# Half of a 31-tap depthwise convolution computed on VectorE instead of TensorE, with gates and output products in another order

## The chip, the cores and the metric

The kernel runs on one core of a Trainium2 chip. The metric is the device time of one execution in microseconds (us). A core has five engines that run beside each other, each with its own in-order queue: PE (TensorE, matrix products), DVE (VectorE), ACT (ScalarE), POOL (GpSimd) and SP (SyncE, which here issues the DMA transfers). Arrays on the chip have 128 partitions; results of PE arrive in PSUM, which has eight banks.

## The reference, cut to what matters

The program is two model blocks for 512 tokens of 1024 features, all in fp32. The change lies in the second block's mixer. Its input projection gives a convolution branch (u_glu), a state space branch (z, xbc, dt) and 2048 gates. The convolution branch is a causal depthwise convolution with 31 taps over 1024 channels:

```python
def conformer_conv_branch(u_glu, glu_b, dw_w, dw_b, ln_g, ln_b, pw_w, pw_b):
    u = u_glu + glu_b
    val, gt = jnp.split(u, 2, axis=-1)
    v = val * jax.nn.sigmoid(gt)
    v = causal_depthwise_conv(v, dw_w, dw_b)          # 31 taps, 1024 channels
    v = jax.nn.silu(layer_norm(v, ln_g, ln_b))        # over all 1024 channels
    return v @ pw_w + pw_b
...
        gates = jax.nn.sigmoid(proj[..., OFF_GATE:] + gate_b[i])
        g_conv, g_ssm = jnp.split(gates, 2, axis=-1)
        conv_out = conformer_conv_branch(...)
        ssm_out = ssd_branch(...)                     # ends in y @ out_w
        mixed = (g_conv * conv_out + g_ssm * ssm_out) @ w_out[i]
```

## The kernel before

Features lie on partitions: a channel tile is 128 channels by 512 tokens, and the convolution has eight of them. Every large product is taken in three matmuls of split operands (mm3, L125): each weight tile of 128x1024 is split by ACT into a high part (L119, L1661) and by POOL into a low part (L121, L1663), with three buffers of each. One projection (proj, L1694) is such a split and 24 matmuls of 512 columns into one PSUM bank; the banks of tag g are two.

The mixer (phase3, L1667) first runs eight groups. Group gi is glu(gi), group(gi) and conv(gi). glu (L1752) is two projections and the gated value vp (L1763); it copies vp into vs, four shifted copies of each block of 32 channels (16 transfers), and builds a block-diagonal weight dw on DVE (L1772). group (L1787) is six projections, a 4-tap convolution on DVE (L1806, L1809) for four of them, and the state space product of four heads, with steps on PE, DVE, ACT and POOL that wait for each other; it ends in two channel tiles of y, stored to memory (L1908). conv (L1776) is 64 matmuls that use 32 columns of PE each, four side by side (L1782), and an evacuation into cv (L1784). The groups' temporary tiles are all in one pool, gw, closed at L1915.

Then come, in the order of the text: the layer norm of cv over channels (L1918 to L1943: a sum over the eight tiles on POOL, a product with ones on PE, centring, squares, a second product with ones, scaling and a silu); sixteen gate projections, whose tanh (L1952) is stored to memory (L1953); the state space branch's out product (gemm_krow, L205, 16 tiles k, with all eight PSUM banks as accumulators), which loads y and the gates back (L1969, L1974); the convolution branch's pointwise product (8 tiles k); and the product with w_out. The out product's inputs are split on ACT and DVE (L224, L226). Around it the residual h is loaded and scaled on DVE (L2005).

The text does not fix the order of the queues. A planner that runs when the program is built simulates it and gives each engine, whenever it is idle there, the ready instruction that stands earliest in the text. Two things tie an order: issue_after (this instruction behind that one in its queue) and keep_in_program_order, which in_order (L191) applies to all of PE's instructions in its scope. A pool opened in the space of a closed pool waits until all of the closed pool is released.

```python
        dw = wk.tile([P, 8, 4, 32], F32, name="dw", tag="dw", bufs=1)
        ...
                nc.tensor.matmul(ps[32 * b:32 * b + 32, :], dw[:, i, b], vs[:, b, 4 * i:4 * i + T],
                                 start=(i == 0), stop=(i == 7), tile_position=(0, 32 * b))
```

Of the kernel before, what the change touches and what calls it, by code (L numbers as in the profile page):

```python
# [109 lines left out]
def split(g, w, shape, pool=None, after=None, hi_on=None):  # L110
# [9 lines left out]
    with tc.issue_after(after[1].ins) if after else nullcontext():  # L120
        (nc.vector if after else nc.gpsimd).tensor_tensor(lv, w, hv, op=OP.subtract)  # L121
# [1459 lines left out]
def p3_loads(g, I, pool):  # L1581
# [4 lines left out]
    for name, items in (  # L1586
# [64 lines left out]
def split_cols(g, w, c, m=P, pool=None):  # L1651
# [10 lines left out]
    with g.tc.issue_after(g.last_hp.ins):  # L1662
        nc.gpsimd.tensor_tensor(wl, wv, wh, op=OP.subtract)  # L1663
# [3 lines left out]
def phase3(g, I, h, out, dbg):  # L1667
# [35 lines left out]
    cv = cvp.tile([P, 8, T], F32, name="cv")  # L1703
    ln_st = ExitStack()
# [4 lines left out]
    gd = [g.dram.tile([P, T], F32, name=f"gTd{i}") for i in range(16)]  # L1709
# [42 lines left out]
    def glu(ct):  # L1752
# [6 lines left out]
        nc.scalar.activation(vb, pv, AF.Identity, bias=tb[:, o_glu + ct:o_glu + ct + 1])  # L1759
        vp = wk.tile([P, 31 + T], F32, name="vp", tag="vp")  # L1760
# [4 lines left out]
        vs = wk.tile([P, 4, VW], F32, name="vs", tag="vs", bufs=1)  # L1765
# [5 lines left out]
        w4 = tdw[ct // 4].rearrange("p (i c) -> p i c", i=8)[:, :, 4 * (ct % 4):4 * (ct % 4) + 4]  # L1771
# [4 lines left out]
    def conv(ct, vd):  # L1776
# [7 lines left out]
        nc.scalar.activation(cv[:, ct], ps, AF.Identity, bias=tb[:, o_dwb + ct:o_dwb + ct + 1])  # L1784

# [133 lines left out]
    nc.gpsimd.tensor_tensor(s1, cv[:, 0], cv[:, 1], op=OP.add)  # L1919
    for k in range(2, 8):  # L1920
        nc.gpsimd.tensor_tensor(s1, s1, cv[:, k], op=OP.add)
    pm = pp.tile([P, 512], F32, name="pln", tag="m")
    nc.tensor.matmul(pm, g.ones, s1, start=True, stop=True)
    s2 = lnp.tile([P, T], F32, name="lns2", tag="s")
    for k in range(8):
        V.scalar_tensor_tensor(cv[:, k], pm, -1.0 / D, cv[:, k], op0=OP.mult, op1=OP.add)
        sq = s2 if k == 0 else lnp.tile([P, T], F32, name="lnsq", tag="t")
        nc.scalar.activation(sq, cv[:, k], AF.Square)
        if k:
            V.tensor_add(s2, s2, sq)  # L1930
    pm = pp.tile([P, 512], F32, name="pln", tag="m")
    nc.tensor.matmul(pm, g.ones, s2, start=True, stop=True)
    rs = lnp.tile([P, T], F32, name="lnr", tag="s")
    nc.scalar.activation(rs, pm, AF.Ln, bias=g.epsl, scale=1.0 / D)
    nc.scalar.activation(rs, rs, AF.Exp, scale=-0.5)
    for k in range(8):
        V.tensor_mul(cv[:, k], cv[:, k], rs)
        th = lnp.tile([P, T], F32, name="lnth", tag="t")
        nc.scalar.activation(th, cv[:, k], AF.Tanh, scale=half[:, o_lng + k:o_lng + k + 1],
                             bias=half[:, o_lnb + k:o_lnb + k + 1])  # L1940
        nc.scalar.activation(cv[:, k], cv[:, k], AF.Identity, scale=tb[:, o_lng + k:o_lng + k + 1],
                             bias=tb[:, o_lnb + k:o_lnb + k + 1])
        V.scalar_tensor_tensor(cv[:, k], th, 1.0, cv[:, k], op0=OP.add, op1=OP.mult)  # L1943
# [12 lines left out]

# [8 lines left out]
    ktp = kt_st.enter_context(tc.tile_pool(name="kt", bufs=2, side="right"))  # L1965

    def yget(k):
        t = ktp.tile([P, T], F32, name="yk", tag="yk", bufs=4)
        nc.sync.dma_start(t, yd[k][:, :])  # L1969
        return t  # L1970

    def gget(i):
        t = ktp.tile([P, T], F32, name="gk", tag="gk", bufs=13)
        nc.sync.dma_start(t, gd[i][:, :])  # L1974
        return t

    gts = {}

    def so_evac(i, ps):
        if dbg is not None and "ssm" in dbg:  # L1980
            t = ktp.tile([P, T], F32, name="dbt", tag="pwt")
            V.tensor_copy(t, ps)
            nc.sync.dma_start(dbg["ssm"][i * P:(i + 1) * P, :], t)
        V.scalar_tensor_tensor(mix[:, i], gts[8 + i], 1.0, ps, op0=OP.add, op1=OP.mult)

    def pw_evac(i, ps):
        t = ktp.tile([P, T], F32, name="pwt", tag="pwt")
        nc.scalar.activation(t, ps, AF.Identity, scale=0.5, bias=tb[:, o_pwb + i:o_pwb + i + 1])
        if dbg is not None and "conv" in dbg:
            nc.sync.dma_start(dbg["conv"][i * P:(i + 1) * P, :], t)  # L1990
# [192 lines left out]
```

## Time and profile before

| | us |
|---|---|
| median of 3 runs (lowest to highest) | 2046.89 (2046.56 to 2046.96) |
| the profiled execution: time | 2046.73 |
| the profiled execution: span from the first to the last instruction | 2045.0 |
| PE busy | 1979.2 |
| DVE busy | 961.5 |
| ACT busy | 702.4 |
| POOL busy | 749.1 |

The rows further down come from one profiled execution. A row's busy time counts from an instruction's start to its end, and ends of neighbours on one engine overlap a little, so that a row of several has less than the sum of its instructions. An idle time is put down to what ended last before the engine went on. A source row gives the least, the median and the largest duration in ns and the first and last start.

### The profile page before, as it was taken

The page shows a single profiled execution, that of the slowest core. Times are in us where ns is not written, and L with a number is a line of the kernel's source. Part 1 is how long each engine was busy: PE and PEld are TensorE (multiplying, and loading weights), DVE is VectorE, ACT ScalarE, POOL GpSimd, SP SyncE. Part 2 cuts the span into 40 slices and gives each one's busy share as a digit, 9 for nine tenths or more (in the row PEclk, how much of TensorE's full clock was granted, in tenths as well). Part 3 has the DMA queues.
Part 4 walks back from the last instruction along what each step waited for, and adds up shares of the span by engine and source line. Part 5 has one row for each costly group of instructions (what it writes and reads, how often), then busy time and mean ns, then how long its engine had stood idle before and what let it go on. Part 6 is the DMA issues. An engine that isn't in the chain of part 4 may idle for free.

```text
span 2045.0 us, 25143 instructions
## 1 busy us (share of the span) xinstructions
PE 1979.2 (97%) x9841; PEld 1396.8 (68%) x9841; DVE 961.5 (47%) x1500; ACT 702.4 (34%) x1057; POOL 749.1 (37%) x490
## 2 busy tenths in 40 slices
PE   7999989799999999989999999999999999999998
PEld 6877637644445545468777777778788888888886
DVE  6266475733444334346776667773545671000112
ACT  5344574411111111153433344443542452222232
POOL 4455453200000000044565555546344444444442
PEclk9999999799999999999999999999999999999999
DMA  4311216299999999845335444434653343332321
GB/s 141 124 42 42 83 42 237 97 399 411 420 420 419 419 419 419 318 140 137 105 114 145 115 118 124 121 106 145 217 184 127 110 113 84 103 98 88 103 83 42
DMA packets 186659, 366.73 MB, mean 179 GB/s; under 512 B 18000, under 2 KB 128888, under 8 KB 161960
## 3 DMA queue, kind: packets, MB, share of 16 engines
q1 hardware_dynamic: 186040, 363.43, 50.0%
q8 instruction: 79, 1.29, 0.3%
q10 hardware_dynamic: 496, 1.64, 0.3%
q14 instruction: 44, 0.36, 0.1%
HBM read 343.54 MB, written 12.65 MB: 174 GB/s over the span
## 4 chain that ended last, share of the span: by engine, by line
PE 64%; DVE 9%; ACT 3%; issue 2%; POOL 2%; SPq 0%; DMA 0%; DVEq 0%; ACTq 0%; POOLq 0%
PE pgu L197 11%; PE psg L126 7%; PE psg L127 7%; PE psg L128 7%; PE py L197 6%; PE pc L197 3%; PE px L197 3%; DVE xacc L1809 2%; PE pcv L1782 2%; DVE G L1878 1%; PE acctr L126 1%; PE accy L126 1%; PE acctr L127 1%; PE acctr L128 1%; PE accy L127 1%
## 5 line engine op out<-in xcount | busy, mean ns | idle before, releaser
L126 PE MATMUL psg<-xh,hi 128*128 128x512 f32 x1040 | 411.5, 396 | 2.5 <-DVE z L1823 2.4
L128 PE MATMUL psg<-xh,lo 128*128 128x512 f32 x1040 | 409.2, 393 | 1.5 <-POOL lo L121 1.5
L127 PE MATMUL psg<-xl,hi 128*128 128x512 f32 x1040 | 406.3, 391 | 0.0
L1663 POOL TENSOR_TENSOR lo<-w,hi 128x1024 fp32r<-128x1024 f32 (+1 forms) x125 | 305.6, 2447 | 239.5 <-ACT hi L1661 233.0
L121 POOL TENSOR_TENSOR lo<-w,hi 128x1024 fp32r<-128x1024 f32 x86 | 210.8, 2456 | 225.8 <-ACT hi L119 224.8
L1661 ACT ACTIVATE hi<-w 128x1024 fp32r<-128x1024 f32 (+1 forms) x125 | 131.1, 1051 | 325.2 <-PE psg L127 227.0
L197 PE MATMUL pgu<-w,xg 128*64 128x512 f32 x1024 | 227.6, 599 | 0.0
L128 PEld LDWEIGHTS psg<-xh,lo 128*128 128x128 f32 x1040 | 195.3, 188 | 44.9 <-issue 2.8
L127 PEld LDWEIGHTS psg<-xl,hi 128*128 128x128 f32 x1040 | 195.4, 188 | 44.2 <-issue 4.7
L126 PEld LDWEIGHTS psg<-xh,hi 128*128 128x128 f32 x1040 | 195.4, 188 | 43.8 <-DVE z L1823 3.4
L1334 POOL TENSOR_TENSOR hh<-x,hh 128x512 fp32r<-128x512 f32 x4 | 5.1, 1275 | 459.6 <-ACT hh L1333 459.6
L197 PEld LDWEIGHTS pgu<-w,xg 128*64 128x64 f32 x1024 | 73.1, 138 | 144.3 <-issue 141.8
L119 ACT CAST hi<-w 128x1024 fp32r<-128x1024 f32 x89 | 92.9, 1044 | 149.5 <-issue 54.8
L197 PE MATMUL py<-w,aT 128*64 128x512 f32 x512 | 113.6, 596 | 0.2 <-ACT aT L1467 0.2
L2105 DVE TENSOR_TENSOR act<-act,psg 128x512 f32<-128x512 f32 x22 | 15.1, 688 | 208.3 <-PE psg L128 203.0
L1459 DVE TENSOR_TENSOR act<-act,pgu 128x512 f32<-128x512 f32 x16 | 11.0, 688 | 187.4 <-PE pgu L197 187.4
L1809 DVE SCALAR_TENSOR_TENSOR xacc<-xp,tsc,xacc 128x512 f32<-128x512 f32 x96 | 90.7, 944 | 2.4
L1322 DVE TENSOR_TENSOR x<-x,pc 128x512 f32<-128x512 f32 x120 | 75.8, 682 | 15.1 <-PE pc L197 14.8
L197 PEld LDWEIGHTS py<-w,aT 128*64 128x64 f32 x512 | 35.4, 137 | 67.6 <-issue 65.4
L1490 ACT ACTIVATE yh<-py,gsl 128x512 fp32r<-128x512 f32 x32 | 22.0, 687 | 138.0 <-PE py L197 138.0
L1806 DVE TENSOR_SCALAR xacc<-xp,tsc,tb 128x512 f32<-128x512 f32 x32 | 49.1, 1534 | 41.5 <-ACT xp L1804 37.0
L1881 POOL TENSOR_TENSOR G<-G,cb 128x512 f32<-128x512 f32 x32 | 50.3, 1588 | 40.0 <-ACT G L1880 25.7
(789 smaller groups left out, 3648.1 us busy)
## 6 DMA issues: line engine op xcount, KB each, us to landing
w<-in_w_expert_down_dram SPq DMA_DIRECT2D x64, 1024.0 KB
w<-in_w_expert_gate_dram SPq DMA_DIRECT2D x64, 1024.0 KB
w<-in_w_expert_up_dram SPq DMA_DIRECT2D x64, 1024.0 KB
w<-in_w_in_dram SPq DMA_DIRECT2D x38, 1024.0 KB
w<-in_w_gate_up_dram SPq DMA_DIRECT2D x44, 512.0 KB
w<-in_w_in_dram SPq DMA_DIRECT2D x32, 512.0 KB
w<-in_w_down_dram SPq DMA_DIRECT2D x11, 1024.0 KB
vs<-vp SPq DMA_DIRECT2D x128, 67.5 KB
```

Source lines behind the costliest of these rows:

```text
L119: (hi_on or nc.scalar.copy)(hv, w)
L121: (nc.vector if after else nc.gpsimd).tensor_tensor(lv, w, hv, op=OP.subtract)
L126: nc.tensor.matmul(ps, ah, bh, start=first, stop=False)
L127: nc.tensor.matmul(ps, ah, bl, start=False, stop=False)
L128: nc.tensor.matmul(ps, al, bh, start=False, stop=last)
L197: return lambda *a, **k: tc.keep_in_program_order(f(*a, **k))
L1322: V.tensor_add(h[:, c, ns], h[:, c, ns], ps)
L1661: nc.scalar.activation(wh, wv, AF.Copy)
L1663: nc.gpsimd.tensor_tensor(wl, wv, wh, op=OP.subtract)
L1806: V.tensor_scalar(acc, xp[:, 0:T], tsc[:, ct:ct + 1], tb[:, o_scb + ct:o_scb + ct + 1], op0=OP.mult, op1=OP.add)
L1809: V.scalar_tensor_tensor(acc, xp[:, k:k + T], tsc[:, 32 * k + ct:32 * k + ct + 1], acc, op0=OP.mult, op1=OP.add)
L1881: nc.gpsimd.tensor_tensor(G, G, cb, op=OP.mult)
```

## The change

Four of the eight channel tiles, 4 to 7, are no longer convolved on PE. glu writes their gated value into one tile, v4, and a generator, late_convs, computes each as 31 steps on DVE: one tensor_scalar with the last tap and the bias, and 30 scalar_tensor_tensor steps that add v4, shifted by d tokens and scaled by the channel's tap, into cv in place. The text calls the generator 4 steps at a time behind each of the first four gate projections, 5 at a time for each tile k of the out product and behind six further gate projections. The gates are no longer stored to memory: those of the convolution branch stay in a tile gcv of pool kt, and those of the state space branch multiply mix at once. So the order of the text becomes: gates 0 and 1 (four projections), the out product, gates 2 to 4, gates 5, the norm's first half, gates 6, its second half, gates 7, the pointwise product; from gates 2 on PE is held in the order of the text. In this stretch, up to the pointwise product, the low parts of weights are computed on DVE (g.lo_on). The residual's scaling and the out product's evacuation move from DVE to ACT. The tap weights of tiles 4 to 7 are loaded with one tap a row. The norm's body keeps its instructions, with two buffers in place of one for its short-lived tile.

```diff
@@ split, split_cols
-        (nc.vector if after else nc.gpsimd).tensor_tensor(lv, w, hv, op=OP.subtract)
+        (nc.vector if after else g.lo_on).tensor_tensor(lv, w, hv, op=OP.subtract)
...
-        nc.gpsimd.tensor_tensor(wl, wv, wh, op=OP.subtract)
+        g.lo_on.tensor_tensor(wl, wv, wh, op=OP.subtract)
@@ p3_loads
-        if name[:3] == "tdw":
-            o = 512 * int(name[3])
+        if name == "tdw0":
             for i in range(8):
...
+        if name == "tdw1":
+            for i in range(4):
+                nc.sync.dma_start(raw[31 * i:31 * i + 31, :], dap(I["conv_dw_w_2"], 512 + P * i, [[D, 31], [1, P]]))
@@ phase3
     cv = cvp.tile([P, 8, T], F32, name="cv")
+    vq = cv_st.enter_context(tc.tile_pool(name="vq", bufs=1))
...
-    gd = [g.dram.tile([P, T], F32, name=f"gTd{i}") for i in range(16)]
@@ glu
+        if ct >= 4:
+            if ct == 4:
+                g.v4 = vq.tile([P, 4, T], F32, name="v4", tag="vs")
+            V.scalar_tensor_tensor(g.v4[:, ct - 4], th, 1.0, vb, op0=OP.add, op1=OP.mult)
+            return None
...
-        vs = wk.tile([P, 4, VW], F32, name="vs", tag="vs", bufs=1)
+        vs = vq.tile([P, 4, VW], F32, name="vs", tag="vs")
@@ behind conv
+    def late_convs():
+        s1 = g.s1 = lnp.tile([P, T], F32, name="lns", tag="s")
+        nc.gpsimd.tensor_tensor(s1, cv[:, 0], cv[:, 1], op=OP.add)
+        for k in (2, 3):
+            nc.gpsimd.tensor_tensor(s1, s1, cv[:, k], op=OP.add)
+        for q_ in range(4):
+            ct, v, w = 4 + q_, g.v4[:, q_], tdw[1][:, 31 * q_:31 * q_ + 31]
+            V.tensor_scalar(cv[:, ct], v, w[:, 30:31], tb[:, o_dwb + ct:o_dwb + ct + 1], op0=OP.mult, op1=OP.add)
+            yield
+            for d in range(1, 31):
+                V.scalar_tensor_tensor(cv[:, ct, d:], v[:, :T - d], w[:, 30 - d:31 - d], cv[:, ct, d:],
+                                       op0=OP.mult, op1=OP.add)
+                yield
+            nc.gpsimd.tensor_tensor(s1, s1, cv[:, ct], op=OP.add)
@@ the loop over groups
-        conv(gi, vp)
+        if vp:
+            conv(gi, vp)
     gw_st.close()
-    s1 = lnp.tile([P, T], F32, name="lns", tag="s")
...
-    for cc in range(8):
-        w = load_cols(g, w2, IN2, [(O_GATE + 256 * cc, 256)])
-        for j in range(2):
-            ct = 2 * cc + j
-            ps = proj(w, j)
-            gt = lnp.tile([P, T], F32, name="gt", tag="gt", bufs=2)
-            nc.scalar.activation(gt, ps, AF.Tanh, scale=0.5, bias=halfg[:, o_gb + ct:o_gb + ct + 1])
-            nc.sync.dma_start(gd[ct][:, :], gt)
...
+    gcv = ktp.tile([P, 8, T], F32, name="gcv", bufs=1)
+    late = late_convs()
+    g.lo_on = V
+    def gates(cs, n):
+        for cc in cs:
+            w = load_cols(g, w2, IN2, [(O_GATE + 256 * cc, 256)])
+            for j in range(2):
+                ct = 2 * cc + j
+                ps = proj(w, j)
+                gt = gcv[:, ct] if ct < 8 else ktp.tile([P, T], F32, name="gt", tag="gt")
+                nc.scalar.activation(gt, ps, AF.Tanh, scale=0.5, bias=halfg[:, o_gb + ct:o_gb + ct + 1])
+                if ct >= 8:
+                    V.scalar_tensor_tensor(mix[:, ct - 8], gt, 1.0, mix[:, ct - 8], op0=OP.add, op1=OP.mult)
+                run(late, n)
@@ so_get, so_evac
-                V.tensor_scalar(h[:, c], h[:, c], q.r1[:, c:c + 1], None, op0=OP.mult)
-        return yget(k)
+                nc.scalar.activation(h[:, c], h[:, c], AF.Copy, scale=q.r1[:, c:c + 1])
+        run(late, 5)
...
-        V.scalar_tensor_tensor(mix[:, i], gts[8 + i], 1.0, ps, op0=OP.add, op1=OP.mult)
+        nc.scalar.activation(mix[:, i], ps, AF.Copy)
@@ behind pw_evac
+    def norm_channels():
+        pm = pp.tile([P, 512], F32, name="pln", tag="m")
+        nc.tensor.matmul(pm, g.ones, g.s1, start=True, stop=True)
...
+        yield
+        pm = pp.tile([P, 512], F32, name="pln", tag="m")
+        nc.tensor.matmul(pm, g.ones, s2, start=True, stop=True)
...
+    gates((0, 1), 4)
     gemm_krow(g, I["ssm_out_w_2"], 16, D, so_get, True, so_evac, B3, tail=2)
+    with in_order(g):
+        gates((2, 3, 4), 5)
+        run(late)
+        norm = norm_channels()
+        gates((5,), 0)
+        run(norm, 1)
+        gates((6,), 0)
+        run(norm, 1)
+        gates((7,), 0)
+    g.lo_on = nc.gpsimd
     gemm_krow(g, I["conv_pw_w_2"], 8, D, lambda k: cv[:, k], True, pw_evac, B3, tail=2)
```

## Rows read from the trace of the kernel before

**Rows 1.** The page's head: busy time of each engine, share of the span, instructions.
```profile
PE 1979.2 (97%) x9841; PEld 1396.8 (68%) x9841; DVE 961.5 (47%) x1500; ACT 702.4 (34%) x1057; POOL 749.1 (37%) x490
```

**Rows 2.** Windows: stretch, its us, busy PE, PEld, DVE, ACT, POOL; clock, DMA.
```profile
1152.00:1436.00 284.00, 278.85 (x1512) 207.96 (x1515) 179.28 (x249) 111.33 (x154) 158.05 (x106) 1.00 0.41 122
...
1396.00:1436.00 40.00, 40.00 (x220) 30.17 (x222) 9.39 (x19) 14.60 (x18) 21.19 (x13) 1.00 0.41 134
```

**Rows 3.** The long convolution on PE: its group, and the last one in the chain.
```profile
L1782 PE MATMUL pcv<-vs,dw 128*32 128x512 f32 x512 | 56.6, 594 | 0.0
...
1431.88 7.00 PE pcv L1782 x64
```

**Rows 4.** A sum's source row; DVE's timeline behind group 7 (start, us, what).
```profile
L1919 POOL TENSOR_TENSOR lns<-cv x1: 2147/2147/2147, 1076.0 to 1076.0; 128x512 f32<-128x512 f32 x1
...
1442.92 3.16 DVE L226 TENSOR_TENSOR kxl<-yk,kxh 128x512 fp32r<-128x512 f32 x3 [6.92 <-DMA yk<-yTd]
1446.16 0.75 DVE L2005 TENSOR_SCALAR h<-h,r 128x1024 f32<-128x1024 f32 x1
...
1448.24 4.87 DVE L1926 SCALAR_TENSOR_TENSOR cv<-pln,cv 128x512 f32<-128x512 f32 x8
```

**Rows 5.** DVE from 1152 to 1436 by group; L1809's source row; a pair.
```profile
L1809 DVE SCALAR_TENSOR_TENSOR xacc<-xp,tsc,xacc 128x512 f32<-128x512 f32 x48 | 47.5, 990 | 1.2
L1806 DVE TENSOR_SCALAR xacc<-xp,tsc,tb 128x512 f32<-128x512 f32 x16 | 24.1, 1507 | 20.6 <-ACT xp L1804 18.4 <-POOL y L1896 2.3
...
L1772 DVE TENSOR_TENSOR dw<-diag,tdw 128x1024 f32<-128x1024 f32 x4 | 9.3, 2318 | 0.0
...
L1809 DVE SCALAR_TENSOR_TENSOR xacc<-xp,tsc,xacc x96: 736/752/2744, 927.8 to 1376.2; 128x512 f32<-128x512 f32 x96
...
1234.69 1.54 DVE L1809 SCALAR_TENSOR_TENSOR xacc<-xp,tsc,xacc 128x512 f32<-128x512 f32 x2
```

**Rows 6.** POOL's and DVE's timelines in the out and pointwise products.
```profile
1509.02 2.39 POOL L121 TENSOR_TENSOR lo<-w,hi 128x1024 fp32r<-128x1024 f32 x1 [2.92 <-ACT hi L119]
1514.45 2.39 POOL L121 TENSOR_TENSOR lo<-w,hi 128x1024 fp32r<-128x1024 f32 x1 [3.04 <-ACT hi L119]
...
1509.50 2.45 DVE L226 TENSOR_TENSOR kxl<-yk,kxh 128x512 fp32r<-128x512 f32 x1 [2.87 <-ACT kxh L224]
...
1617.96 0.69 DVE L226 TENSOR_TENSOR kxl<-mix,kxh 128x512 fp32r<-128x512 f32 x1
```

**Rows 7.** Timelines of PE, ACT and SP, and y's stores, at group 7's end.
```profile
1384.64 0.40 PE L128 MATMUL psg<-xh,lo 128*128 128x512 f32 x1
...
1393.56 0.67 ACT L1952 ACTIVATE gt<-psg,halfg 128x512 f32<-128x512 f32 x1
...
1428.16 0.67 ACT L1952 ACTIVATE gt<-psg,halfg 128x512 f32<-128x512 f32 x1
...
L1908 SPq DMA_DIRECT2D yTd<-y x16: 319/326/339, 1009.7 to 1436.0; - x16
...
1439.04 1.74 SPq L1969 DMA_DIRECT2D yk<-yTd  x4
```

**Rows 8.** The norm's two sums on PE, in the chain that ended last.
```profile
1445.46 0.86 PE pln L1923 x2
...
1468.36 0.86 PE pln L1932 x2
```

**Rows 9.** Waits from 1384.6 to 1436 us: in total, times, longest.
```profile
DVE G L1878 <- PE py L1883: 8.1, 1, 8.1
DVE y L1894 <- PE py L1883: 4.6, 1, 4.6
...
DVE xd L1835 <- PE px L1831: 3.9, 1, 3.9
...
DVE S L1860 <- PE pst L1853: 2.8, 2, 1.6
```

**Rows 10.** A window of five us in which PE was nearly idle (columns as in rows 2).
```profile
885.00:890.00 5.00, 0.09 (x1) 0.12 (x1) 3.79 (x11) 2.24 (x7) 2.61 (x3) 0.66 0.26 105
```

More of the change, by code (lines that the diff above doesn't have):

```diff
@@ L1770, in glu @@
         dw = wk.tile([P, 8, 4, 32], F32, name="dw", tag="dw", bufs=1)
[L1771 removed]
+        w4 = tdw[0].rearrange("p (i c) -> p i c", i=8)[:, :, 4 * ct:4 * ct + 4]
         V.tensor_tensor(dw, g.diag32[:, None, None, :].to_broadcast([P, 8, 4, 32]),
@@ L1965, in phase3 @@
     ktp = kt_st.enter_context(tc.tile_pool(name="kt", bufs=2, side="right"))
[L1967 to L1983, printed above, removed]
-        V.scalar_tensor_tensor(mix[:, i], gts[8 + i], 1.0, ps, op0=OP.add, op1=OP.mult)
[L1986 to L1990, printed above, removed]
-        V.scalar_tensor_tensor(t, gts[i], 1.0, t, op0=OP.add, op1=OP.mult)
-        V.tensor_add(mix[:, i], mix[:, i], t)
-    for i in range(8):
-        gts[8 + i] = gget(8 + i)
-    for i in range(8):
-        gts[i] = gget(i)
+    gcv = ktp.tile([P, 8, T], F32, name="gcv", bufs=1)
[12 more added lines that the diff above has]
+                run(late, n)
     def so_get(k):
@@ L2004, in so_get, with so_evac @@
             for c in range(NT):
-                V.tensor_scalar(h[:, c], h[:, c], q.r1[:, c:c + 1], None, op0=OP.mult)
-        return yget(k)
-    gemm_krow(g, I["ssm_out_w_2"], 16, D, so_get, True, so_evac, B3, tail=2)
+                nc.scalar.activation(h[:, c], h[:, c], AF.Copy, scale=q.r1[:, c:c + 1])
+        run(late, 5)
+        t = ktp.tile([P, T], F32, name="yk", tag="yk", bufs=4)
+        nc.sync.dma_start(t, yd[k][:, :])
+        return t
+    def so_evac(i, ps):
+        if dbg is not None and "ssm" in dbg:
+            t = ktp.tile([P, T], F32, name="dbt", tag="pwt")
+            V.tensor_copy(t, ps)
+            nc.sync.dma_start(dbg["ssm"][i * P:(i + 1) * P, :], t)
+        nc.scalar.activation(mix[:, i], ps, AF.Copy)
@@ new lines, in pw_evac @@
+    def pw_evac(i, ps):
+        t = ktp.tile([P, T], F32, name="pwt", tag="pwt")
+        nc.scalar.activation(t, ps, AF.Identity, scale=0.5, bias=tb[:, o_pwb + i:o_pwb + i + 1])
+        if dbg is not None and "conv" in dbg:
+            nc.sync.dma_start(dbg["conv"][i * P:(i + 1) * P, :], t)
+        V.scalar_tensor_tensor(t, gcv[:, i], 1.0, t, op0=OP.add, op1=OP.mult)
+        V.tensor_add(mix[:, i], mix[:, i], t)
+    def norm_channels():
+        pm = pp.tile([P, 512], F32, name="pln", tag="m")
+        nc.tensor.matmul(pm, g.ones, g.s1, start=True, stop=True)
+        s2 = lnp.tile([P, T], F32, name="lns2", tag="s")
+        for k in range(8):
+            V.scalar_tensor_tensor(cv[:, k], pm, -1.0 / D, cv[:, k], op0=OP.mult, op1=OP.add)
+            sq = s2 if k == 0 else lnp.tile([P, T], F32, name="lnsq", tag="t", bufs=2)
+            nc.scalar.activation(sq, cv[:, k], AF.Square)
+            if k:
+                V.tensor_add(s2, s2, sq)
+        yield
+        pm = pp.tile([P, 512], F32, name="pln", tag="m")
+        nc.tensor.matmul(pm, g.ones, s2, start=True, stop=True)
+        rs = lnp.tile([P, T], F32, name="lnr", tag="s")
+        nc.scalar.activation(rs, pm, AF.Ln, bias=g.epsl, scale=1.0 / D)
+        nc.scalar.activation(rs, rs, AF.Exp, scale=-0.5)
+        for k in range(8):
+            V.tensor_mul(cv[:, k], cv[:, k], rs)
+            th = lnp.tile([P, T], F32, name="lnth", tag="t", bufs=2)
+            nc.scalar.activation(th, cv[:, k], AF.Tanh, scale=half[:, o_lng + k:o_lng + k + 1],
+                                 bias=half[:, o_lnb + k:o_lnb + k + 1])
+            nc.scalar.activation(cv[:, k], cv[:, k], AF.Identity, scale=tb[:, o_lng + k:o_lng + k + 1],
+                                 bias=tb[:, o_lnb + k:o_lnb + k + 1])
+            V.scalar_tensor_tensor(cv[:, k], th, 1.0, cv[:, k], op0=OP.add, op1=OP.mult)
+        yield
@@ L2138, in tile_kernel @@
     make_consts(g)
-    g.wi, g.ringb = 0, None
+    g.wi, g.ringb, g.lo_on = 0, None, nc.gpsimd
     g.ring = g.ring_st.enter_context(tc.tile_pool(name="ring", bufs=RA))
```

27 lines of the change are left out of this document (1 added, 26 removed).

## Prediction

> **What bounds the kernel now.** Start with the page's head: PE is busy 97% of the span [rows 1]. The stage that the change touches runs from about 900 to 1630 us; there the windows show PE at 278.85 of the 284 us from the fifth group's start (1152) to the end of group 7 (1436), and without a gap in the last 40 [rows 2]. So work taken from PE there is worth its full time as long as nothing else becomes late. The same rows show VectorE (DVE) at 179.28 of the 284 us and GpSimd (POOL) at 158.05. Next, the price of the work that moves: one channel tile's convolution stands 7.00 us on PE in the chain that ended last, and the eight sum to 56.6 us [rows 3]. Last, the order of the queues, which decides here. The planner starts whatever is ready on an engine that it sees idle, however late it is written: the sum over conv tiles (L1919), written behind all eight groups, runs at 1076.0 us, and on DVE the split of the first out-product inputs (L226) and the residual's scaling (L2005) run at 1442.92 and 1446.16, ahead of the layer norm's L1926 that is written before both [rows 4].
>
> **PE's saving.** Four of eight convolutions leave PE, half of 56.6: 28.3 us [rows 3]. With nothing late this would be the whole answer, 2046.7 - 28.3 = 2018.4.
>
> **Where the 124 DVE steps go.** They are written under the gates and the out product, 4 or 5 after each projection. But a step needs only v4 of its channel tile, which glu(4) to glu(7) write, and no tie holds it back. By [rows 4] I take them to start in groups 4 to 7, where DVE is idle for 284 - 179.3 = 104.7 us [rows 2]. Price of a step: the nearest row is L1809, an instruction of the same kind and shape that also feeds its own result back, among the same neighbours: mean 990 ns in this window, 736 at least [rows 5]. Two such in a row start 0.80 us apart (1.54 - 0.74 [rows 5]), whereas independent ones of L1926 start 0.60 apart ((4.87 - 0.68) / 7 [rows 4]); so a dependent step costs some 0.05 over its duration. A step covers 497 of 512 columns on average, 3% of its 0.52 us or so of streaming less, 0.016. Thus 120 x (0.99 + 0.05 - 0.016) = 123 us, and four first steps like L1806 at 1.51 make 6: 129 us. Away go four builds of the matmul weights (L1772), 9.3 us [rows 5]. DVE's demand in the window is 179.3 - 9.3 + 129 = 299 us against 284. **Term one: the end of group 7 comes 15 us later than now**, and the 28.3 us of PE turn into PE waiting for DVE.
>
> The bounds of that term. If no step meets POOL, it costs 0.775 (0.74 + 0.05 - 0.016), 120 of them 93 and the four first ones, at the same price at most, 3: with 179.3 - 9.3 that is 266 us, DVE is not the bound, and group 7 ends at best 28 us earlier. The other bound is from what POOL does to DVE: L226 takes 0.69 us at 1617.96 but 2.45 at 1509.50, when it starts just behind POOL's 2.39 us subtraction, and it ends after that [rows 6]. If every POOL instruction shuts DVE out so, only 44% (1 - 158/284) of the 104.7 idle us can be used, 46 us, and 96 - 9 - 46 = 41 us are left over. I take 15, from the row of the same instruction in the same stretch, and keep -28 and +41.
>
> **The tail of group 7.** From the last z projection (1384.64) until group 7's results are stored (1436.0) PE is now filled with gate projections: six are evacuated from 1393.56 to 1428.16 [rows 7]. The new gate outputs lie in pool kt, opened in the space of the groups' pool, which must be released whole; that such a wait is real shows in the first load into kt, at 1439.04, behind the last store of y at 1436.0 [rows 7]. So before the release only two gate projections can run, as many as there are banks of tag g, and four move behind it. A projection is 24 matmuls, as one k of the out product is, and the subtractions of successive k start 5.43 us apart [rows 6]: 4 x 5.43 = 21.7 us. Of the last convolution 2.9 us ran after 1436.0 (1431.88 + 7.00 [rows 3]); they go. The start behind the release costs 3.0 us (1439.04 - 1436.0) and a tanh of 0.67 like L1952's [rows 7] with some 0.6, my estimate, for its handover: 4.3. **Term two: 21.7 - 2.9 + 4.3 = 23 us.**
>
> **The layer norm** is now held in PE's order: its second sum (now L1932's) stands behind gates 6. Today it takes from 1445.46 to 1468.36, 22.9 us, beside four other projections [rows 8]; the new cover is two, 10.9 us. DVE needs 15 steps of 0.60 to 0.69, about 10 us, plus ACT's last square and the handovers. **Term three: 3 us** of PE waiting, between 0 and 12 (22.9 - 10.9).
>
> **Edits at nothing.** The 32 transfers of gates to memory and back, and the 64 shifted copies of four tiles, leave SP's queue; PE waits for neither now. The 32 subtractions that move from POOL to DVE cost there at most two of L226's 0.69 [rows 6], 1.38, beside 5.43 us of PE for each; with the convolution done by then they are hidden. If the steps are still there, 5 x 0.775 + 1.38 + 0.69 = 5.95 per k is 0.5 over PE, 8 us for 16 k. The residual's scaling and the out product's evacuation go to ACT, which is busy 111 of the 284 us in the groups [rows 2] and does no more than a split and a copy per k later.
>
> **Sum.** The profiled execution took 2046.73 us, 0.16 under the median of 2046.89; its span is 2045.0 [rows 1]. 2046.7 + 15 + 23 + 3 = 2087.7; I say 2088. Its own range: -28 + 23 + 0 = -5 gives 2042, and +41 + 23 + 3 = +67 gives 2114.
>
> **Rivals.** *The steps stay where they are written* (faster, 0.20). For it: the text spaces them by hand, 4 or 5 per projection. Against: [rows 4]. Then PE gains its 28.3 us and the tail decides. PE has some 10 us of group 7's own work there and two projections, 11. The dependent chain now takes 51.4 us (1384.6 to 1436.0), of which DVE waited 8.1 + 4.6 + 3.9 + 2.8 = 19.4 for results that queued on PE behind projections [rows 9]; without these it is 32, and the hole 32 - 21 = 11: 2046.7 - 28.3 + 11 + 4.3 + 3 = 2037. It decides while the hole is under some 17 us (28.3 - 4.3 - 3, less the 4 us that can be told).
> *They stay, but the hole and DVE's pace eat the gain* (same, 0.08): a hole of 13 and the 8 us above, 2046.7 - 28.3 + 13 + 4.3 + 3 + 8 = 2047. In both, the change does what it says, and my first step does not happen.
> *POOL shuts DVE out whole* (slower still, 0.12): every dense step meets every POOL instruction, as L226 does in [rows 6], and the time is 2114. Against it: L1809's mean is only 0.25 us over its least [rows 5]. PE's idle stretches would add to it: in five us with 0.09 of PE the granted clock was 0.66 [rows 10]. The Trainium skill (SBUF — State Buffer, "SBUF: two separate sides") says that the port pair shared by the two engines is locked for the whole instruction and the loser "fully blocks". [Rows 6] agree; by that rule with dense steps the sum would be 2114, by the row of L1809 it is 2088.
>
> **How the numbers follow.** The main case has 0.60, the rivals 0.20, 0.08 and 0.12. What a measurement here can tell from no change is about 0.2%, 4 us. Faster is the first rival and the low corner of the main case, 0.21; same 0.08; slower 0.71. The range of 2033 to 2114 reaches from 4 us under the first rival's price to the full shut-out; some 0.1 lies below and 0.1 above.
>
> **What would show it.** Right: DVE's late steps begin before group 5 ends; from group 5 on DVE is near full and PE under 90%; group 7's last store comes later than 1436; at most two gate projections run before it; after it PE is full but for a wait at the norm's second sum. Wrong: the steps first start after group 7 (then the hole in its tail is the number to read), or they take 0.78 us among POOL's work with PE still full, which leaves 2046 or less.

## The result, and the profile after

| | us |
|---|---|
| after: median of 4 runs (lowest to highest) | 2109.35 (2108.51 to 2111.26) |
| before, beside it on the same chip: median of 4 runs | 2046.93 (2046.56 to 2047.9) |
| ratio, 95% interval | 1.0309 (1.0295 to 1.0322) |
| after: span of the profiled execution | 2108.2 |

The change costs 62.4 us. The forecast was 2088 (2033 to 2114). PE is busy for almost as long as before, in a longer span, although 256 matmuls of the convolution, 28.3 us [rows 3], are gone (compare [rows 1]). From the page's head:

```profile
PE 1977.4 (94%) x9585; PEld 1405.2 (67%) x9585; DVE 1058.0 (50%) x1648; ACT 708.0 (34%) x1065; POOL 683.0 (32%) x450
```

The windows of the kernel after, with the columns of [rows 2]: first from the fifth group's start to the last store of y, then the stretch in it where DVE is fullest, and then the parts ahead of the first late step and behind the last one.

```profile
1152.00:1464.30 312.30, 251.27 (x1173) 194.28 (x1171) 280.34 (x374) 102.77 (x141) 147.84 (x94) 0.89 0.28 85
1250.00:1438.00 188.00, 145.12 (x620) 113.64 (x619) 184.28 (x245) 61.84 (x86) 85.65 (x54) 0.85 0.27 84
...
1152.00:1202.80 50.80, 49.44 (x279) 35.91 (x278) 37.27 (x51) 22.20 (x31) 29.26 (x22) 1.00 0.41 122
...
1438.80:1464.30 25.50, 13.59 (x72) 9.68 (x71) 11.08 (x21) 7.41 (x10) 10.90 (x8) 0.80 0.12 41
```

In 188 us DVE is busy for 184 and PE for 145, at a granted clock of 0.85. PE's matmuls take longer there: those of L126 for projections have a mean of 416 ns from 1152 to 1464, where from 1152 to 1436 they had 399 before. What DVE does stands in its groups from 1152 to 1464 us (name, count, busy us, mean ns, idle us before it and what ended it):

```profile
L1806 DVE SCALAR_TENSOR_TENSOR cv<-v,tdw,cv 128x511 f32<-128x511 f32 (+20 forms) x120 | 133.2, 1116 | 1.2
L1834 DVE SCALAR_TENSOR_TENSOR xacc<-xp,tsc,xacc 128x512 f32<-128x512 f32 x48 | 44.5, 928 | 0.4
...
L1831 DVE TENSOR_SCALAR xacc<-xp,tsc,tb 128x512 f32<-128x512 f32 x16 | 17.9, 1119 | 6.4 <-ACT xp L1829 6.3
...
L1932 DVE SCALAR_TENSOR_TENSOR y<-y,half,rs 128x512 f32<-128x512 f32 x10 | 7.0, 745 | 11.6 <-ACT rs L1929 11.6
```

All 120 late steps are in that list, although the text writes them behind the groups. The source rows (least, median and largest duration in ns, first and last start) say when they ran and when y was stored:

```profile
L1806 DVE SCALAR_TENSOR_TENSOR cv<-v,tdw,cv x120: 708/732/2972, 1202.8 to 1438.8; 128x511 f32<-128x511 f32 x4, 128x510 f32<-128x510 f32 x4, 128x509 f32<-128x509 f32 x4, 128x508 f32<-128x508 f32 x4
...
L1933 SPq DMA_DIRECT2D yTd<-y x16: 319/338/345, 1010.8 to 1464.3; - x16
```

The last store comes at 1464.3 us instead of 1436.0 [rows 7]: **28.3 us late**. The rest lies behind it: from that store to the end of the span it was 2045.0 - 1436.0 = 609.0 us before and is 2108.2 - 1464.3 = 643.9 now, **34.9 us more**. PE's timeline after shows two gaps there (start, duration, what, and in brackets the wait):

```profile
1467.20 0.79 PE L126 MATMUL psg<-xh,hi 128*128 128x512 f32 x1 [7.03 <-ACT gcv L1964]
1467.79 0.63 PE L127 MATMUL psg<-xl,hi 128*128 128x512 f32 x1
...
1471.50 0.39 PE L127 MATMUL psg<-xl,hi 128*128 128x512 f32 x1
...
1628.71 2.08 PE L197 MATMUL pln<-lns,ones 128*128 128x512 f32 x2 [6.08 <-DVE lns L2006]
```

The first gap ends when the pool is free and the first gate can be evacuated into it, 2.9 us behind the last store. The second is the norm's second sum. Behind the first gap ten matmuls take 4.3 us, 1467.20 to 1471.50, where ten at full clock take 2.3. The windows of those ten and of the 28 us behind them:

```profile
1467.20:1471.40 4.20, 4.20 (x10) 3.33 (x11) 0.69 (x1) 1.15 (x2) 0.00 (x0) 0.51 0.88 280
1472.00:1500.00 28.00, 28.00 (x125) 23.21 (x124) 9.32 (x10) 13.33 (x16) 0.00 (x0) 1.00 0.62 223
```

The granted clock is 0.51 first, the lower of its two levels (1.2 GHz), and then 1.00, the higher (2.4 GHz); before it PE had waited for 7.03 us. What else is longer is work. These are the windows of the gate projections alone (tile psg; PE's busy time and its matmuls come first), for the kernel before from its last store to its last pointwise evacuation:

```profile
1436.00:1629.40 193.40, 52.47 (x224) 41.97 (x224) 0.00 (x0) 6.75 (x10) 1.00 0.47 162
```

and for the kernel after, likewise:

```profile
1464.30:1692.80 228.50, 80.67 (x336) 64.99 (x336) 0.00 (x0) 10.67 (x16) 0.97 0.36 121
```

336 matmuls are 14 projections of 24, 224 are 9.33: 4.67 projections have moved behind the release.

### The profile page after: what moved, and what is told of

Same layout as the page of the kernel before. It is cut to its first block, busy times and chain, and to the rows that moved or that the text cites. A ratio compares the mean times of both kernels' runs of the same rounds, so it can differ in the third digit from the quotient of the medians.

```text
span 2108.2 us, 24554 instructions
## 1 busy us (share of the span) xinstructions
PE 1977.4 (94%) x9585; PEld 1405.2 (67%) x9585; DVE 1058.0 (50%) x1648; ACT 708.0 (34%) x1065; POOL 683.0 (32%) x450
## 5 line engine op out<-in xcount | busy, mean ns | idle before, releaser
L126 PE MATMUL psg<-xh,hi 128*128 128x512 f32 x944 | 378.5, 401 | 30.3 <-DVE z L1848 12.7
L128 PE MATMUL psg<-xh,lo 128*128 128x512 f32 x944 | 376.5, 399 | 1.5 <-POOL lo L121 1.5
L127 PE MATMUL psg<-xl,hi 128*128 128x512 f32 x944 | 375.0, 397 | 0.0
L1666 POOL TENSOR_TENSOR lo<-w,hi 128x1024 fp32r<-128x1024 f32 (+1 forms) x109 | 270.0, 2479 | 233.6 <-ACT hi L1664 231.3
L121 POOL TENSOR_TENSOR lo<-w,hi 128x1024 fp32r<-128x1024 f32 x70 | 173.5, 2483 | 350.1 <-ACT hi L119 349.1
L126 PEld LDWEIGHTS psg<-xh,hi 128*128 128x128 f32 x944 | 181.1, 192 | 73.2 <-DVE z L1848 14.8
L128 PEld LDWEIGHTS psg<-xh,lo 128*128 128x128 f32 x944 | 180.7, 191 | 41.8 <-issue 2.2
L127 PEld LDWEIGHTS psg<-xl,hi 128*128 128x128 f32 x944 | 180.8, 192 | 39.0 <-issue 1.9
L1806 DVE SCALAR_TENSOR_TENSOR cv<-v,tdw,cv 128x511 f32<-128x511 f32 (+20 forms) x120 | 133.2, 1116 | 1.2
```

What stands on the lines that cost most here:

```text
L121: (nc.vector if after else g.lo_on).tensor_tensor(lv, w, hv, op=OP.subtract)
L126: nc.tensor.matmul(ps, ah, bh, start=first, stop=False)
L127: nc.tensor.matmul(ps, ah, bl, start=False, stop=False)
L128: nc.tensor.matmul(ps, al, bh, start=False, stop=last)
L1666: g.lo_on.tensor_tensor(wl, wv, wh, op=OP.subtract)
L1806: V.scalar_tensor_tensor(cv[:, ct, d:], v[:, :T - d], w[:, 30 - d:31 - d], cv[:, ct, d:], op0=OP.mult, op1=OP.add)
```

## The experiments

| kernel | us | ratio to before (95%) | last store of y |
|---|---|---|---|
| before | 2046.93 | 1 | 1436.0 |
| after | 2109.35 | 1.0309 (1.0295 to 1.0322) | 1464.3 |
| convolution part alone | 2088.99 | 1.0204 (1.0187 to 1.0222) | 1483.9 |
| order alone | 2067.80 | 1.0101 (1.0083 to 1.0119) | 1420.6 |
| steps tied behind group 7 | 2053.62 | 1.0035 (1.0022 to 1.0048) | 1410.5 |
| 120 steps left out | 2057.60 | 1.0052 (1.0034 to 1.0069) | 1412.3 |
| low parts zero in groups 4 to 7 | 2062.03 | 1.0080 (1.0062 to 1.0098) | 1415.6 |
| low parts on DVE in groups 4 to 7 | 2081.40 | 1.0168 (1.0148 to 1.0188) | 1437.0 |
| tied, six gates in the tail | 2049.56 | 1.0015 (1.0006 to 1.0025) | 1425.0 |
| the same, later second sum | 2049.10 | 1.0019 (1.0010 to 1.0029) | 1422.6 |
| tied, eight gates in the tail | 2049.60 | 1.0017 (1.0007 to 1.0027) | 1422.3 |
| the same, 31 steps free | 2046.55 | 1.0001 (0.9991 to 1.0010) | 1437.7 |
| the same, 62 steps free | 2065.62 | 1.0096 (1.0081 to 1.0112) | 1455.0 |
| the same, 62 steps tied behind cb | 2046.96 | 1.0006 (0.9997 to 1.0016) | 1435.2 |

Times are medians; the kernel before had medians of 2045.64 to 2046.93 beside them. The last column is from each profiled execution, which took up to 4.3 us more than the median (six gates in the tail: 2053.88), so differences of a few us between two such executions carry no weight.

### Which half of the change costs what

**The convolution part alone**, in the kernel before: v4, late_convs and the tap weights for it; gates, norm and order stay as they were.

```diff
-        conv(gi, vp)
+        if vp:
+            conv(gi, vp)
...
-    s1 = lnp.tile([P, T], F32, name="lns", tag="s")
...
+    run(late_convs())
+    s1 = g.s1
```

> The kernel before with the convolution's part of the change alone: channels 512 to 1023 on VectorE, written behind the groups; the gates, their way through memory, the norm, the low parts on GpSimd and the order stay. Theory (two separate losses): the steps start in groups 4 to 7 here too, the last store of y comes 20 to 35 us after 1436.0, and since six or so gate projections still fill the tail, the loss there is all: 2060 to 2085 us. Rival (the loss is in the order of gates, norm and out product alone): 2047 or less.

**The order alone**: the kernel after with all eight channel tiles on PE.

```diff
-        if ct >= 4:
...
-            return None
...
-        for q_ in range(4):
...
+        for k in range(2, 8):
```

> The changed kernel's order (gates kept in SBUF, the norm behind the out product, the low parts on VectorE) with all eight channel tiles convolved on PE as before. Theory: the tail of group 7 and the norm cost 25 to 36 us by themselves, 2072 to 2083, with the last store of y at 1425 to 1440 and no gate evacuated before it. Rival (VectorE's load made the tail, and the order costs nothing with PE's convolutions): 2035 to 2052.

The stores of y, of the convolution part alone:

```profile
L1933 SPq DMA_DIRECT2D yTd<-y x16: 319/338/347, 1009.0 to 1483.9; - x16
```

and of the order alone:

```profile
L1916 SPq DMA_DIRECT2D yTd<-y x16: 319/332/339, 1009.6 to 1420.6; - x16
```

Alone, the convolution part costs 42.2 us (2088.99 - 2046.77) and the order 21.0 (2067.80 - 2046.77); together 63.2, and the whole change costs 62.4. So there are two separate losses that nearly add up, and neither rival holds. But both sizes were expected otherwise. The steps cost more: they move the last store by 47.9 us from before (1483.9 - 1436.0), and by 43.7 from the order alone to after. The order costs less, because the gate projections that leave the tail let group 7 end 15.4 us sooner, and 36.2 us come back behind it (2065.8 - 1420.6 = 645.2 against 609.0).

### Is it the place of the steps?

**Tied**: each channel tile's first step may start only behind group 7's last scaling of y.

```diff
-            V.tensor_scalar(cv[:, ct], v, w[:, 30:31], ...)
+            with tc.issue_after(g.last_y.ins):
+                V.tensor_scalar(cv[:, ct], v, w[:, 30:31], ...)
...
-            V.scalar_tensor_tensor(ys[j], ys[j], ...)
+            g.last_y = V.scalar_tensor_tensor(ys[j], ys[j], ...)
```

> The changed kernel with one edit: the first VectorE step of each late channel may start only behind group 7's last scaling of y on VectorE. Theory (the steps' early start in groups 4 to 7 costs the stage its PE saving): the steps run under the gates and the out product, the last store of y falls from 1464.3 to 1408 to 1425 us, PE is back over 95% busy in groups 4 to 7, and the time is 2048 to 2070 us (2109 less 40 to 56; what stays above 2018 is the tail of group 7 and the norm). Rival (the order of gates, norm and out product is the loss, the steps only happen to lie there): 2095 or more. Second rival (the steps do not fit under the out product either): store early as above, but PE waits between the out product and the norm's first sum, and the time stays above 2080.

**Steps left out**: 120 of the 124 are not computed.

```diff
-            for d in range(1, 31):
+            for d in ():
```

> Leaves out 120 of the 124 VectorE steps of the late channels: only the first tap with the bias is computed for channels 512 to 1023. Theory (the steps load VectorE in groups 4 to 7): last store of y at 1400 to 1420 us and the time 2043 to 2065, within 8 us of the kernel with the steps tied behind group 7. Rival (the order is the loss): 2095 or more. If this is over 10 us faster than the tied kernel, the steps cost something under the out product and the gates too.

Of the tied kernel: the source row of the steps, that of the stores, and two windows.

```profile
L1807 DVE SCALAR_TENSOR_TENSOR cv<-v,tdw,cv x120: 711/728/1754, 1412.2 to 1524.8; 128x511 f32<-128x511 f32 x4, 128x510 f32<-128x510 f32 x4, 128x509 f32<-128x509 f32 x4, 128x508 f32<-128x508 f32 x4
...
L1934 SPq DMA_DIRECT2D yTd<-y x16: 320/332/339, 1010.3 to 1410.5; - x16
...
1240.00:1330.00 90.00, 83.75 (x395) 67.25 (x395) 62.29 (x84) 38.43 (x54) 50.05 (x34) 0.98 0.39 115
1330.00:1410.00 80.00, 64.45 (x309) 50.58 (x307) 50.45 (x79) 30.07 (x41) 32.16 (x23) 0.91 0.25 82
```

The tie takes back 55.7 us. Under the out product the steps cost nothing that can be told, since the kernel without them is no faster. So the place of the steps is what the change as written loses most by. Still the tied kernel is slower than before: of 28.3 us of PE's work taken away, it gains 14.2 on the order alone (2067.80 - 2053.62). The theory's 95% for PE was wrong: PE has 6.3 us of gaps in the first window and 15.6 in the second; before, with the convolutions and the gates to run, it had 2.5 (90 - 87.49) and 1.2 (80 - 78.78) in the same two stretches.

### Why a step is dear in the groups

In the tied kernel the median step takes 728 ns and few take more. In the kernel after the median is 732, but the mean is 1116. Its DVE timeline shows one late step take 2.74 us, and the same three instructions of L1903 take 2.81 us and 0.67:

```profile
1301.21 2.74 DVE L1806 SCALAR_TENSOR_TENSOR cv<-v,tdw,cv 128x482 f32<-128x482 f32 x1
...
1305.83 2.81 DVE L1903 TENSOR_SCALAR G<-ab,acs 128x128 f32<-128x128 f32 x3
...
1321.32 0.67 DVE L1903 TENSOR_SCALAR G<-ab,acs 128x128 f32<-128x128 f32 x3
```

and its POOL timeline what ran beside the step and beside the first three (beside the second three POOL stood idle), and POOL's groups what there is of it from 1152 to 1464 us:

```profile
1300.62 2.81 POOL L1666 TENSOR_TENSOR lo<-w,hi 128x1024 fp32r<-128x1024 f32 x1
...
1305.32 2.85 POOL L1666 TENSOR_TENSOR lo<-w,hi 128x1024 fp32r<-128x1024 f32 x1
...
L1666 POOL TENSOR_TENSOR lo<-w,hi 128x1024 fp32r<-128x1024 f32 x28 | 74.4, 2658 | 43.3 <-ACT hi L1664 43.3
```

**Low parts zero**: ACT writes them in groups 4 to 7, POOL does not subtract.

```diff
-        g.lo_on.tensor_tensor(wl, wv, wh, op=OP.subtract)
+        if getattr(g, "zero_lo", False):
+            nc.scalar.activation(wl, wv, AF.Copy, scale=0.0)
+        else:
+            g.lo_on.tensor_tensor(wl, wv, wh, op=OP.subtract)
...
+        g.zero_lo = gi >= 4
```

> The changed kernel, but in groups 4 to 7 ScalarE writes zeros for the low parts of the projections' weights where GpSimd subtracted them: that leaves out the weights' low part there. Theory (a late step among GpSimd's work takes 1.116 us in the mean, against 0.73 in the tied kernel while GpSimd stands idle, because the two engines hold each other up): the mean falls to 0.95 or less, the last store of y comes 15 us earlier than 1464.3 or more, and the time is 2075 to 2097. Rival (VectorE is late by the number of instructions in its queue and by waits, not by their price): the mean falls by less than 0.08 and the time stays within 6 us of 2109.

Its group of the steps, from 1152 to 1416 us, and its window to the last store:

```profile
L1809 DVE SCALAR_TENSOR_TENSOR cv<-v,tdw,cv 128x503 f32<-128x503 f32 (+18 forms) x120 | 103.2, 865 | 1.2
...
1152.00:1415.60 263.60, 235.88 (x1148) 185.56 (x1146) 227.35 (x373) 126.56 (x166) 68.25 (x64) 0.93 0.32 96
```

The mean falls by 0.25 us, the stores end 48.7 us sooner, and the kernel is 47.3 us faster, more than the theory gave it. As this kernel also leaves arithmetic out, the next leaves nothing out.

**Low parts on DVE**, in the kernel after, from group 4 on.

```diff
     for gi in range(8):
+        if gi == 4:
+            g.lo_on = V
         vp = glu(gi)
```

> The changed kernel with one edit, nothing left out: from group 4 on the low parts of the projections' weights are subtracted on VectorE, in 1.22 us each, where GpSimd takes 2.66. Theory (the late steps are dear because GpSimd's 28 subtractions hold VectorE up): VectorE's own load is the 227 us of the kernel with zero low parts and 28 x 1.22 = 34 more, 262, with the 36 us of idle time it had there 298, so the last store of y comes at 1440 to 1452 instead of 1464.3 and the time is 2085 to 2097: work put onto the overloaded engine makes the kernel faster. Rival (VectorE is simply over-full, and the zero low parts helped by sparing the projections a wait): 34 us more on it, last store after 1480, 2125 or more.

Its DVE groups, its stores, and its window from 1152 us to the last of them:

```profile
L1806 DVE SCALAR_TENSOR_TENSOR cv<-v,tdw,cv 128x511 f32<-128x511 f32 (+19 forms) x120 | 104.7, 878 | 1.2
L1666 DVE TENSOR_TENSOR lo<-w,hi 128x1024 fp32r<-128x1024 f32 x32 | 43.1, 1348 | 1.3 <-ACT hi L1664 1.3
...
L1933 SPq DMA_DIRECT2D yTd<-y x16: 319/338/906, 1012.0 to 1437.0; - x16
...
1152.00:1437.00 285.00, 245.41 (x1174) 190.60 (x1173) 265.01 (x402) 103.12 (x141) 78.06 (x66) 0.92 0.30 93
```

28 more subtractions, some 38 us (28 x 1.35), put on the engine that is already full make the kernel 28 us faster and the stage 27.3 us shorter, both a little more than the theory's ranges (2085 to 2097, and 1440 to 1452 for the last store). Without its subtractions (43.1 and one of 1.2) DVE is busy for 220.7 us here, against 280.3 - 6.4 = 273.9 in the kernel after: 53.2 us less, while POOL is busy for 69.8 less (147.84 - 78.06). A us of POOL's beside a nearly full DVE took 0.76 us of it; by the kernel with zero low parts it is 0.66 (273.9 - 221.2 = 52.7 for 147.84 - 68.25 = 79.6), and both are rough, as POOL's spans are. The rival is refuted. No run moved the subtractions without the late steps. Where PE sets the pace they have less to give: with the order alone PE is busy for 256.1 of the 268.6 us to the last store, so at most some 12.5 us could come back there.

### Can the saving be kept?

Six kernels tried to, all on the tied one. The first three fill the tail of group 7 with gate projections again, whose gates go through memory as before.

```diff
     gw_st.close()
+    for cc in range(3):
+        w = load_cols(g, w2, IN2, [(O_GATE + 256 * cc, 256)])
+        for j in range(2):
...
+            nc.sync.dma_start(gd[ct][:, :], gt)
...
-    gates((0, 1), 4)
...
+    for i in range(6):
+        nc.sync.dma_start(gcv[:, i], gd[i][:, :])
```

**Six gates in the tail**:

> The tied kernel, with six of the gate projections written ahead of the pools' release again, as in the kernel before: their gates go to memory and are loaded back into the gate tile behind the out product's loads. Theory (PE stands idle in the tail of group 7 because nothing is left to fill it): the tied kernel's PE is idle for 6.3 + 15.6 + 3.4 us from 1240 to 1440, so 15 to 28 us go and the time is 2025 to 2039. Rival (the filling projections hold up group 7's own matmuls by as much): 2045 or more, with the last store of y 15 us later than 1410.5.

Its stores, and PE's waits from 1152 to 1480 us (in total, times, longest):

```profile
L1935 SPq DMA_DIRECT2D yTd<-y x16: 319/325/339, 1013.7 to 1425.0; - x16
...
PE acctr L126 <- ACT kxh L224: 11.6, 1, 11.6
PE psg L126 <- DVE z L1850: 7.5, 3, 3.3
```

This is the rival: PE is full in the tail, the last store moves by 14.5 us, and a new wait of 11.6 stands behind it, for the out product's first input. The time falls by 4 us only.

**The second sum of the norm one projection later**:

> As the kernel with six gates in the tail, and the norm's second sum stands one projection later in PE's order, half of gates 7 ahead of it and half behind. Theory (PE waits 6.1 us at the second sum because one projection pair covers 11 us of the norm's 17): the wait falls under 2 us and the time by 3 to 6 us against the kernel without this edit. Rival (the wait moves behind, to the first input of the pointwise product): within 2 us of it.

PE's waits from 1480 to 1700 us:

```profile
PE acctr L126 <- ACT kxh L224: 5.1, 1, 5.1
PE pln L197 <- DVE lns L2018: 0.7, 1, 0.7
```

The rival again. The wait of 6.1 becomes 0.7, and 5.1 us come back at the pointwise product.

**Eight gates in the tail**:

> As the kernel with the later second sum, but with eight gate projections ahead of the release. Theory (the hole holds some 25 us of projections besides the two that ran there, 36 us in all, which six of 5.4 us nearly fill): within 4 us of the kernel with six, either a gain of the last few us of the hole, or a loss at the norm's first sum, which then has one projection pair less to wait for VectorE's steps that end near 1525. Rival (the hole takes all eight): 6 us faster or more.

PE's waits in its two stretches, 1152 to 1480 and 1480 to 1700 us:

```profile
PE psg L126 <- DVE z L1850: 7.5, 3, 3.4
PE pm L1928 <- POOL sq L1926: 2.8, 4, 0.8
PE acctr L126 <- ACT kxh L224: 2.5, 1, 2.5
PE px L1858 <- DVE u L1841: 1.5, 2, 0.7
...
PE pln L197 <- POOL lns L1811: 9.0, 1, 9.0
PE acctr L126 <- ACT kxh L224: 6.0, 1, 6.0
```

As the theory had it, there is no gain: the gap has moved to the norm's first sum, where DVE's last step is late. The list also accounts for most of the lost 28.3 us. The six waits are 29.3 us, and the kernel before has 5.1 such in the first stretch and none behind it: 24.2 are new. That slow matmuls behind each wait make up the rest is not shown; the granted clock from 1480 to 1700 us is 0.96.

The last three let some steps start sooner, with the norm's sums earlier in PE's order.

```diff
-            with tc.issue_after(g.last_y.ins):
+            with tc.issue_after(g.last_y.ins) if q_ >= 1 else nullcontext():
```

**31 steps free**:

> As the kernel with eight gates in the tail, but the first late channel tile's 31 steps are not tied (they may start in groups 4 to 7), and the norm's sums stand one projection earlier and two projections earlier in PE's order. Theory (what is left over the PE's work is DVE's lateness behind group 7: 9.0 us of PE at the norm's first sum, 6.0 at the pointwise product's first input): 31 steps fewer there, at 0.66 each, are 20 us, both waits go, and the 31 steps fit into the 105 us that VectorE has free in the groups: 2030 to 2038, faster than before by 8 us or more. Rival (even 31 steps among GpSimd's subtractions hold up the groups' own chains): the last store of y at 1432 or later instead of 1422.3, and 2044 or more.

**62 steps free** (q_ >= 2):

> As the kernel with one channel tile's steps free, with two of them free. Theory: behind group 7 nothing is left to gain, and 62 steps at 1.1 us are 68 of the 105 us that VectorE has free in the groups, without the steps that come too late for them: 2030 to 2046, no faster than with one. Rival (VectorE's price in the groups does not matter while its share is under full): 5 us or more faster than with one.

The stores of the kernel with 31 free:

```profile
L1935 SPq DMA_DIRECT2D yTd<-y x16: 319/338/345, 1010.2 to 1437.7; - x16
```

and with 62:

```profile
L1935 SPq DMA_DIRECT2D yTd<-y x16: 319/332/345, 1009.0 to 1455.0; - x16
```

With none free the last store is at 1422.3, with 31 at 1437.7, with 62 at 1455.0: half a us of the stage for each step, for the first 31 as for the next. The gain behind group 7 is there (PE waits 1.3 us instead of 15.0 ahead of and in the pointwise product, to which the sums' earlier place may add), and the 31 steps give it back. That was the rival, and the theory that DVE's idle time in the groups would take them for nothing is wrong; with 62 the time, 2065.6, is also far above the 2030 to 2046 expected. But the free steps do not spread over that idle time. The windows from 1200 to 1250 us, with 31 free and with none (the kernel with eight gates):

```profile
1200.00:1250.00 50.00, 45.72 (x216) 36.92 (x215) 49.50 (x59) 11.63 (x18) 26.04 (x13) 0.97 0.29 83
...
1200.00:1250.00 50.00, 49.24 (x245) 40.16 (x244) 32.87 (x47) 19.87 (x28) 28.68 (x18) 1.00 0.36 109
```

The 31 start as soon as their input is there, from 1200.7 to 1252.3, and DVE, which had 17 us free in these 50, is full. Whether steps spaced out over the groups would cost less was not tested.

**62 steps behind cb**, the mask product of group 7, and so only in the tail's waits:

```diff
+            with tc.issue_after((g.last_y if q_ >= 2 else g.last_cb).ins):
```

> As the kernel with one channel tile's steps free, but the steps of the first two late channel tiles are tied behind the mask product (cb) of group 7 and the other two behind its last scaling: none of them meets the groups' convolution taps, and some 40 steps fall into VectorE's 29 us of waiting between 1387 and 1421. Theory (the price of a step is where it stands: among the taps and GpSimd's weight subtractions it is paid twice, in the tail's waits it is nearly free): the last store of y stays at 1422 to 1430, PE's 15 us behind group 7 in the kernel with eight gates go, and the time is 2030 to 2040, faster than before by 6 us or more. Rival (also there the steps hold up the chain they stand in, one step for each wait): the last store at 1432 or later and 2044 or more.

Its stores, and PE's waits from 1152 to 1480 us:

```profile
L1935 SPq DMA_DIRECT2D yTd<-y x16: 319/326/339, 1008.3 to 1435.2; - x16
...
PE acctr L126 <- ACT kxh L224: 8.5, 1, 8.5
PE psg L126 <- DVE z L1850: 7.5, 3, 3.3
PE pm L1928 <- POOL sq L1926: 7.0, 5, 4.2
```

That was the rival: also here the chain that ends in the last store is held up, by 12.9 us against the kernel with eight gates, and again the steps run in a bunch: DVE is busy for all 50 us from 1386 to 1436. No version was faster than the kernel before; two of them (31 free, 62 behind cb) cannot be told from it.

## Why the prediction was right, and where its sizes were off

**Right.** The late steps start in groups 4 to 7 (first at 1202.8), DVE is full there and PE at 145 of 188 us, the last store comes later, at most two gate projections run ahead of the release (PE waits 7.03 us for the first of them to be evacuated behind it), and behind it PE is full but for the norm's second sum. Undoing this one placement takes back 55.7 of the 62.4 us. The time came out 21 us over the forecast, and that is in two terms.

**Term one, 15 us, measured 28.3.** The step that failed is the comparison of demand and time: "DVE's demand in the window is ... 299 us against 284". The demand was 280.3, less than that. Late and first steps together were dearer, 136.2 us where I took 129 (a late step 1.116 where I took 1.024), and five subtractions on DVE add 6.4. But the other rows were cheaper than before, 156.6 us for 177.5 (L1831's 17.9 us where its counterpart had 24.1 [rows 5]). And I added the steps' durations to a busy time, in which neighbours overlap: all rows of the window add up to 18.9 us more than the busy time, where before it was 7.5. So 299 + 7.2 + 6.4 - 20.9 - 11.4 is 280.3. What I left out is that DVE cannot use the whole window: it waited for 312.3 - 280.3 = 32.0 us, 11.6 of them for rs, 6.3 for xp. 13.5 of the 32.0 lie ahead of the first late step (50.80 - 37.27), 14.4 behind the last (25.50 - 11.08), where what is left of group 7's chain still takes 25.5 us. 280.3 - 299 + 32.0 is 13.3 us over the forecast. The deeper fault is that I treated DVE's 104.7 idle us as room. The runs with 0, 31 and 62 free steps show a price of half a us each, while DVE has idle time left further on: ready steps fill it in a bunch and hold up the chain there.

**What POOL does to DVE** I put at 0.99 us a step by L1809's row, and gave 0.12 to a rival by which every instruction of POOL's shuts DVE out, 2114. The price of that rival is nearer to the result than mine, in part by luck: of my miss of 21 us some 9 lie behind the last store, of which that rival says nothing. The two kernels without POOL's subtractions show the mechanism to be worth more than half of the 43.7 us that the steps cost beside the order: the stage is 27 us shorter even with that work on DVE. It is not whole, at 0.66 to 0.76 us of DVE for one of POOL. The Trainium skill (SBUF — State Buffer, "SBUF: two separate sides") says that of two such instructions the one that starts first has the shared port pair for the whole instruction, and the other "fully blocks". The timeline agrees with that where a late step meets a subtraction (2.74 us against a median of 0.73), and the sum of busy times stays under it.

**Terms two and three, 26 us, measured 35.1** from the last store to the last pointwise evacuation (228.5 - 193.4). Four projections were counted, 21.7 us, and 4.67 moved, 25.3. The start behind the release was put at 4.3 and is 2.9. The last convolution's 2.9 go, as forecast. The norm's wait was put at 3 and is 6.1. What was not in the sum is the clock behind both gaps: 2.0 us for the first ten matmuls at 1467.20, and at 1628.71 two sums in 2.08 where the first two took 0.86, with some 0.5 in the matmuls that follow, 3.7 together. 25.3 + 2.9 - 2.9 + 6.1 + 3.7 = 35.1.

The two terms are not alone in the sense I gave them. By itself the order costs 21.0 us, since group 7 ends 15.4 sooner when the gates leave its tail. I gave the order no such credit, and it is there beside the steps too: from the convolution part alone to the kernel after, the last store comes 19.6 us sooner (1483.9 - 1464.3). So term one's 28.3 is a difference, 43.7 for the steps less 15.4 for the emptier tail.

**The rival that the steps stay where they are written, 2037,** is the tied kernel, 2053.6. Its gap of 11 us in the tail, and 4.3 for the start behind it, was too small: from 1240 to 1440 PE is idle for 25.2 us in the tied kernel (6.3, 15.6 and 3.4 in three windows), and a part of that lies ahead of the tail, where groups without a convolution have nothing to put under the wait for DVE's z (7.4 us of PE in the tied kernel). The step "the hole 32 - 21 = 11" failed there. The norm's 3 is 6.1 here too.

**Edits at nothing** held as far as they were tested: the 120 steps beside the low parts' subtractions on DVE delay the out product by nothing that can be told (2053.6 with them, 2057.6 without). The transfers that went and ACT's new work were not tested by themselves.

## What to carry to other kernels

Idle time of an engine, as a sum over a stage, is not yet room for new work when the engine stands inside a chain that another engine waits for: a planner that starts what is ready puts the new work there in a bunch. Ask for each new instruction which waiting instruction it comes ahead of, and tie it behind the chain if it is not urgent. Work taken from the bound engine is worth its time only where something else is ready to fill the gap; here the convolutions were that filling, and in the kernel with eight gates 24 of 28 us came back as waits. Before moving work onto DVE, count what POOL does beside it, and try moving POOL's part too, even onto the full engine.

## What the runs showed of the hardware that was not expected

Putting some 38 us of subtractions on a DVE that was busy 184 of 188 us made its stage 27 us shorter, because POOL's 2.66 us versions of them had cost it more. A step that feeds its own result back shows hardly a price for that when four channel tiles alternate. These are seven steps in a row of the tied kernel, where they alternate, and two of the kernel with 31 free, both of one channel tile:

```profile
1412.21 4.71 DVE L1807 SCALAR_TENSOR_TENSOR cv<-v,tdw,cv 128x511 f32<-128x511 f32 x7
...
1221.05 1.50 DVE L1808 SCALAR_TENSOR_TENSOR cv<-v,tdw,cv 128x497 f32<-128x497 f32 x2
```

The seven start (4.71 - 0.74) / 6 = 0.66 us apart, the two 1.50 - 0.73 = 0.77. And PE's granted clock fell to 0.85 over the 188 us in which PE was still busy for 145. DVE waited for only 3.7 us in that stretch, so there a slower PE can hardly have lengthened the stage. What the clock of 0.80 cost in the 25.5 us behind the last late step was not separated from the waits and stays open.
